# Grouped-query attention on one core: weighted sums redistributed between the score tiles, VectorE's correction steps moved behind the copy of the transposes, V loaded over four jobs

## The chip, the cores and the metric

The kernel runs on one core of a Trainium2 chip. The core's engines run side by side, each with its own queue of instructions, which it works through in order: PE (TensorE, matmuls), DVE (VectorE), ACT (ScalarE), POOL (GpSimd) and SP (SyncE, which issues DMAs here). Data lies in HBM, in SBUF (128 partitions) or in PSUM, to which PE writes. The metric is the device time of one execution in microseconds (us), lower is better. Before the change the median of three runs is 431.78 us (431.51 to 432.28).

## What is computed

Q has shape (8, 512, 32, 64): batch, sequence, heads, dimension. K and V have 8 heads, and four heads of Q share one head of K and V:

```python
K_expanded = np.repeat(K, heads_per_group, axis=2)
V_expanded = np.repeat(V, heads_per_group, axis=2)
...
scores = np.einsum('bhqd,bhkd->bhqk', Q, K_expanded) * scale
weights = np.exp(scores - np.max(scores, axis=-1, keepdims=True))
weights = weights / (np.sum(weights, axis=-1, keepdims=True) + 1e-10)
...
output = np.einsum('bhqk,bhkd->bhqd', weights, V_expanded)
```

There is no mask. scale is 1/8.

## The kernel before

**Jobs.** `fast_path` works through 64 jobs. A unit `u` is a batch `b` and a pair `gp` of K/V heads; job `j` is unit `j // 2` and one head `g = j % 2` of the pair, with its four heads of Q as two pairs `i`. One batch is eight jobs. The scores are made transposed (keys on the partitions), so that their exponentials can be the stationary operand of the matmul with V without another transpose. The maximum isn't subtracted; instead the row sums and V are checked to be in bounds, and a slow general path, not run here, follows if they aren't.

**Tiles of a job.** A job has 16 score pieces of 128 keys x 512 queries. ScalarE takes 14 of them, two at a time, as seven tiles: `act_tile(j, n)` issues two matmuls (L209) into `s_ps`, of which there are two buffers, and one exponential (L227) from there into `pt`. The other two pieces go to VectorE. From job 10 on every second job is *wide*: VectorE takes three pieces, and ScalarE's tile 4 has one piece only. The other jobs are called narrow. A wide job is followed by a narrow one.

**VectorE's exponentials.** `exp_d` issues the matmuls of these pieces into `d_ps` and turns them into 16-bit integers `u` (L238), whose bits read as an approximate exponential. `exp_d2` cuts out the mantissa, `f` (L259). GpSimd makes a correction from it, `g` (L251) and `w` (L255); in jobs 0 to 2 and 63 VectorE does this itself. `exp_d4` adds `u` and `w` into `pt` (L272); for job `j` this stands in job `j + 1`. The two steps `f` and `pt` read and write only SBUF.

**PSUM for it.** `d_ps` has one buffer of two banks. A job uses it twice: for the pieces of `exp_d`, then for the transposes of a later job's Q (`trans_q`, L164, copied to `qt` at L167), in the first batch also for K's (`first_k`), and, when `g` is 0, for a check of V (`check_v`, L177, reduced into `okv` at L184). The third piece of a wide job is put into its second bank in the job before.

**Weighted sums.** For job `j - 1`, called `last`, `pv(last, i, lo, hi)` issues matmuls `lo` to `hi` of 32 for head pair `i` (L303), each with a block of `pt` as the stationary operand and 65 columns of V, the last of which is ones and gives the row sum. `pv` has one buffer of two banks. The matmuls of pair 1 take the keys in the order 2, 3, 1, 0; a wide job's blocks from the 16th on, and a narrow job's from the 24th on, need `exp_d4`. `norm(last, i)` follows on VectorE: reciprocal `inv` (L336), product `o_sb` (L340), and after every second job the store by SP. After every eighth job (after pair 1 of jobs 7, 15, 23 ..., so at the end of jobs 8, 16, 24 ...) two small VectorE steps (L314) check 128 columns of `inv` against bounds; they read and write SBUF.

**Order.** The order is written out by hand, and each engine keeps it. In a job of the steady state PE's queue is, with n for `act_tile(j, n)`: 0, pieces of `exp_d`, 1, 11 weighted sums of pair 0, 2, 11 more, 3, 10 more, 4, transposes (and check, and the third piece of the next job), 5, 16 of pair 1, 6, 16 more. VectorE's queue is: `u`, `pt` of the last job, `f`, `norm` of pair 0, copy of the transposes, `okv`, the next job's third `u`, `norm` of pair 1. GpSimd issues the loads of Q, K and V as DMAs, from its own queue and ahead of the job's `g` and `w`: one load of Q per unit, in the third job of a batch the next batch's K, in the fourth its V as four loads of 128 KB. SP transposes the next batch's K by DMA in the fifth job (`dma_k`).

Of the kernel before, what the change touches and what calls it, by code (L numbers as in the profile page):

```python
# [11 lines left out]
FP32 = mybir.dt.float32  # L12
BF16 = mybir.dt.bfloat16
FP16 = mybir.dt.float16
I16 = mybir.dt.int16
U16 = mybir.dt.uint16
I32 = mybir.dt.int32
ALU = mybir.AluOpType
# [15 lines left out]
VV_HI = 1.0e30  # L34
# [24 lines left out]
def fast_path(ctx, tc, Q, K, V, out, flag):  # L59
    nc = tc.nc  # L60
    B, S, H, D = Q.shape
    KV = K.shape[2]
    HPG = H // KV
    SC = S // 128
    GP = KV // 2
    NU = B * GP
# [6 lines left out]
    const_pool = ctx.enter_context(tc.tile_pool(name="const", bufs=1))  # L73
# [13 lines left out]

    ident = const_pool.tile([128, 128], BF16, name="ident")
    ok = const_pool.tile([128, SPB * 2 * SC], FP32, name="ok")
    okv = const_pool.tile([128, NU + 1], FP32, name="okv")  # L90
    okall = const_pool.tile([128, 1], FP32, name="okall")
    gate = const_pool.tile([1, 1], FP16, name="gate")
    warm = const_pool.tile([128, S], BF16, name="warm")
# [6 lines left out]
    def load_k(b, lo=0, hi=KV):  # L100
        if b not in kn:
            kn[b] = knat_pool.tile([128, SC, KV, D], BF16, name="k_nat")
        nc.gpsimd.dma_start(
            out=kn[b][:, :, lo:hi, :],
            in_=K[b, :, lo:hi, :].rearrange("(sc p) g d -> p sc g d", p=128),
        )


    def load_v(b, lo=0, hi=KV):
        for sc in range(SC):  # L110
            nc.gpsimd.dma_start(  # L111
                out=vt[b % 2][:, sc, lo:hi, 0:D],
                in_=V[b, sc * 128:(sc + 1) * 128, lo:hi, :],
            )
# [16 lines left out]
    def d_tile():  # L131
        return d_pool.tile([128, 2, S], FP32, name="d_ps")
# [60 lines left out]
    def taken(j):  # L193
        return 3 if WIDE(j) else 2
# [22 lines left out]
    def open_job(j):  # L217
        pt = pt_pool.tile([128, NPAIR, SC, 2, S], FP16, name="pt")
        jobs.setdefault(j, {}).update(pt=pt, pv={})

    def act_tile(j, n):
        group = act_tiles(j)[n]
        i, kc, lo = group[0]
        ps = s_pool.tile([128, 2, S], FP32, name="s_ps")
        for _, _, m in group:
            scores(j, ps[:, m, :], i, kc, m)
        nc.scalar.activation(  # L227
            out=jobs[j]["pt"][:, i, kc, lo:, :], in_=ps[:, lo:, :], func=EXP, scale=scale
        )

    def exp_d(j, lo, hi, ps):
        st = jobs.setdefault(j, {})
        if "u" not in st:
            for name, dtype in (("u", I16), ("f", I16), ("g", BF16), ("w", BF16)):
                st[name] = dve_pool.tile([128, 3, S], dtype, name=name + "16")[:, 0:taken(j), :]
        for n in range(lo, hi):
            scores(j, ps[:, n - lo, :], DPAIR, n // 2, n % 2)
        return lambda: nc.vector.tensor_scalar(  # L238
            out=st["u"][:, lo:hi, :], in0=ps[:, 0:hi - lo, :], scalar1=A_U, scalar2=B_U,
            op0=ALU.mult, op1=ALU.add,  # L240
        )


    def by_pool(j):
        return 3 <= j < NJOB - 1
# [3 lines left out]
    def correction(engine, f, g, w):  # L249
        as_bits = engine is nc.gpsimd  # L250
        engine.tensor_scalar(  # L251
            out=g, in0=f, scalar1=-EXP_F1, scalar2=EXP_K * 2.0 ** (24 * as_bits),
            op0=ALU.add, op1=ALU.mult,
        )
        engine.tensor_tensor(out=w, in0=g, in1=f.bitcast(FP16) if as_bits else f, op=ALU.mult)  # L255

    def exp_d2(j):
        st = jobs[j]
        nc.vector.tensor_single_scalar(  # L259
            out=st["f"], in_=st["u"], scalar=1023, op=ALU.bitwise_and  # L260
        )
        if by_pool(j):
            exp_d3(j, nc.gpsimd)

    def exp_d3(j, engine):
        st = jobs[j]
        correction(engine, st["f"], st["g"], st["w"])

    def exp_d4(j):
        st = jobs[j]  # L270
        n = taken(j)
        nc.vector.tensor_tensor(  # L272
            out=st["pt"][:, DPAIR, :, :, :].rearrange("p kc m q -> p (kc m) q")[:, 0:n, :].bitcast(
                U16
            ),
            in0=st["u"],
            in1=st["w"],
            op=ALU.add,
        )
# [8 lines left out]
    def pv(j, i, lo, hi):  # L288
        st = jobs[j]
        u, g = divmod(j, 2)  # L290
        b, gp = divmod(u, GP)
        if lo == 0:

            if j < NJOB - 1:
                t = pv_pool.tile([128, 2, S], FP32, name="pv")
            else:
                t = d_tile() if i == 0 else s_pool.tile([128, 2, S], FP32, name="s_ps")
            t = t.rearrange("p m (qc c) -> p m qc c", qc=SC)
            st["pv"][i] = t[:, :, :, 0:D + 1]
        order = blocks(j, i)  # L300
        for n in range(lo, hi):
            kc, m, qc = order[n]
            nc.tensor.matmul(  # L303
                st["pv"][i][:, m, qc, :],
                st["pt"][:, i, kc, m, qc * 128:(qc + 1) * 128],
                vt[b % 2][:, kc, 2 * gp + g, :],
                start=(n < 2 * SC and qc == 0),
                stop=(n >= len(order) - 2 * SC and qc == SC - 1),
            )
# [73 lines left out]
        )  # L383


    def probe():
        f = const_pool.tile([128, 2], I16, name="probe_f")
        g = const_pool.tile([128, 2], BF16, name="probe_g")
        w = const_pool.tile([128, 2], BF16, name="probe_w")
        nc.gpsimd.memset(f, 512)  # L390
        correction(nc.gpsimd, f, g, w)
        nc.vector.tensor_scalar(
            out=okv[:, NU:NU + 1], in0=w[:, 0:1], scalar1=-80.0, scalar2=2.0 * VV_HI,
            op0=ALU.is_gt, op1=ALU.mult,
        )


    load_k(0, 0, 2)
    load_q(0, (0, 2, 4, 8))
    make_identity(nc, ident)  # L400
# [13 lines left out]
    bank = d_tile()  # L414
# [4 lines left out]
    bank = d_tile()  # L419
# [3 lines left out]
    for j in range(NJOB):  # L423
        end = j == NJOB - 1
        last = j - 1
        late = last >= 0
        u, g = divmod(j, 2)
        b, gp = divmod(u, GP)
        open_job(j)
        if j == 1:  # L430

            nc.gpsimd.tensor_copy(out=gate, in_=jobs[0]["pt"][0:1, 0, SC - 1, 0, 0:1])
            load_q(2)
            load_q(3)
            probe()
        if g == 0 and u >= 1 and u + 3 < NU:
            load_q(u + 3)
        if gp == 1 and b + 1 < B:
            if g == 0:
                load_k(b + 1)  # L440
            else:
                load_v(b + 1)
        if gp == 2 and g == 0 and b + 1 < B:
            dma_k(b + 1)
        act_tile(j, 0)
        if j == 0:
            trans_q(0, bank[:, 1, :], 1, NPAIR)()
            act_tile(j, 1)
            exp_d(j, 0, 2, d_tile())()
        else:  # L450
            exp_d(j, 0, 2, d_tile())()
            act_tile(j, 1)
        if late:
            pv(last, 0, 0, 11)
        act_tile(j, 2)
        if late and by_pool(last):
            exp_d4(last)
        exp_d2(j)
        if late:
            pv(last, 0, 11, 22)  # L460
        act_tile(j, 3)
        if late:
            pv(last, 0, 22, 32)
            norm(last, 0)
        act_tile(j, 4)

        reads = []
        if not end:
            bank = d_tile()

            ahead = (j + 1,) if j < 7 else (8, 9) if j == 7 else (j + 2,)
            for n, to in enumerate(ahead):
                if to < NJOB:
                    reads.append(trans_q(to, bank[:, n, :]))
            if j == 1:
                for swap in range(2):
                    reads.append(first_k(1, swap, bank[:, 1, swap * S // 2:]))
            elif j > 1 and b == 0 and gp + 1 < GP:
                reads.append(first_k(gp + 1, g, bank[:, 1, :]))
            if g == 0 and u > 0:  # L480
                reads.append(check_v(u - 1, bank[:, 1, S // 2:]))
            if j == NJOB - 2:
                reads.append(check_v(u, bank[:, 1, S // 2 + D:]))
            if taken(j + 1) > 2:
                reads.append(exp_d(j + 1, 2, taken(j + 1), bank[:, 1:2, :]))
        else:
            pv(j, 0, 0, 16)
        for read in reads:
            read()
        if not by_pool(j):  # L490
            exp_d3(j, nc.vector)
            exp_d4(j)
        act_tile(j, 5)
        if late:
            pv(last, 1, 0, 16)
        act_tile(j, 6)
        if late:
            pv(last, 1, 16, 32)
            norm(last, 1)
            del jobs[last]  # L500
        if end:
            pv(j, 0, 16, 32)
            norm(j, 0)
            pv(j, 1, 0, 32)
            norm(j, 1)
# [118 lines left out]
```

## Time and profile before

| What | Value |
|---|---|
| median of 3 runs | 431.78 us (431.51 to 432.28) |
| profiled execution | 433.24 us |
| its span, first to last instruction | 431.6 us |
| granted TensorE clock, mean | 0.995 |
| ACT busy | 407.5 us, 94% |
| PE busy | 395.4 us, 92% |
| DVE busy | 337.0 us, 78% |
| POOL busy | 292.7 us, 68% |
| exponentials L227 | 448, 406.2 us busy, 15.8 us idle before them |
| weighted sums L303 | 178.7 us busy |
| moved by DMA | 66.97 MB, mean 155 GB/s |

The span is what the profile's rows add up to; the profiled execution's time also has what lies around it, and the median is that of other executions. A row of the timeline has a start, a length, the engine, the line, the operation, what it writes and reads, how many instructions are merged into it, and in brackets the engine's idle time before it and what ended it. Rows of PE overlap, because matmuls are pipelined: the distance between two starts tells more than a length.

### The profile page before, as it was taken

To read this page: it belongs to the slowest core of one execution; us is meant where nothing else is said; L and a number is where in the kernel's file an instruction comes from. 1 tells how busy PE (TensorE), PEld (TensorE's weight loads), DVE (VectorE), ACT (ScalarE), POOL (GpSimd) and SP (SyncE) were. 2 spreads that over 40 slices of the span, in tenths; PEclk is the share of its full clock that TensorE was granted. 3 is DMA by queue.
4 is the path that set the end of the run, shared out by engine and by line. 5 is a ranking of instruction groups with operands and counts; after the bars stand their busy time and mean duration, and the time that the engine had idled before them with its cause. 6 is when DMAs were issued, how large, how long until landed. Compare 5 with 4: busy or idle time off the path is not lost.

```text
span 431.6 us, 13558 instructions
## 1 busy us (share of the span) xinstructions
PE 395.4 (92%) x5945; PEld 245.1 (57%) x5945; DVE 337.0 (78%) x612; ACT 407.5 (94%) x449; POOL 292.7 (68%) x212
## 2 busy tenths in 40 slices
PE   7888999999999999999999999999999999999994
PEld 2455565555556555556555556556555555655653
DVE  1687778878888878878878877887887887887875
ACT  2989999999999999999999999999999999999993
POOL 8805564896679776697676977599666987657650
PEclk9999999999999999999999999999999999999997
DMA  9998656799349966399846989569975998622214
GB/s 105 185 151 183 169 141 145 131 172 235 117 136 197 177 165 150 107 218 147 236 81 149 193 134 260 141 108 172 202 169 145 188 156 196 150 99 99 99 62 140
DMA packets 91439, 66.97 MB, mean 155 GB/s; under 512 B 52080, under 2 KB 74608, under 8 KB 91376
## 3 DMA queue, kind: packets, MB, share of 16 engines
q0 software_dynamic: 56544, 25.17, 50.4%
q1 hardware_dynamic: 34832, 40.90, 34.5%
q8 instruction: 47, 0.77, 0.8%
q14 instruction: 16, 0.13, 0.1%
HBM read 50.33 MB, written 33.55 MB: 194 GB/s over the span
## 4 chain that ended last, share of the span: by engine, by line
ACT 48%; PE 37%; DVE 10%; issue 3%; POOL 1%; ACTq 0%; DVEq 0%; POOLq 0%
ACT pt L227 48%; PE s_ps L209 15%; PE pv L303 11%; PE d_ps L164 8%; DVE o_sb L340 3%; DVE u L238 2%; PE d_ps L177 2%; PE d_ps L209 2%; DVE ok L314 1%; DVE pt L272 1%; DVE f L259 1%; DVE inv L336 1%; DVE w L255 0%; POOL q_nat L126 0%; DVE qt L167 0%
## 5 line engine op out<-in xcount | busy, mean ns | idle before, releaser
L227 ACT ACTIVATE pt<-s_ps 128x1024 f16<-128x1024 f32 (+1 forms) x448 | 406.2, 1032 | 15.8 <-PE s_ps L209 15.5
L303 PEld LDWEIGHTS <-pt 128*128 128x128 f16 x4096 | 142.7, 98 | 89.5 <-issue 57.1
L303 PE MATMUL pv<-v,pt 128*128 128x65 bf16 x4032 | 178.7, 195 | 9.0 <-DVE o_sb L340 4.6
L209 PE MATMUL s_ps<-qt,kt 64*128 64x512 bf16 x757 | 157.4, 382 | 15.6 <-ACT pt L227 1.8
L255 POOL TENSOR_TENSOR w<-g,f 128x1024 bf16<-128x1024 bf16 (+1 forms) x60 | 153.8, 2564 | 5.0
L251 POOL TENSOR_SCALAR g<-f 128x1024 bf16<-128x1024 int16 (+1 forms) x60 | 74.0, 1234 | 118.6 <-DVE f L259 118.2
L238 DVE TENSOR_SCALAR u<-d_ps 128x1024 int16<-128x1024 f32 (+1 forms) x91 | 96.0, 1055 | 0.7 <-PE d_ps L209 0.7
L340 DVE TENSOR_TENSOR o_sb<-pv,inv 128x512 f32<-128x512 f32 x125 | 86.4, 691 | 4.3
L209 PEld LDWEIGHTS <-kt 64*128 64x128 bf16 x896 | 55.1, 93 | 51.4 <-issue 18.5
L336 DVE RECIPROCAL inv<-pv 128x8 f32<-128x8 f32 x125 | 25.8, 206 | 52.7 <-PE pv L303 51.8
L167 DVE COPY qt<-d_ps 128x1024 bf16<-128x1024 bf16 (+1 forms) x65 | 44.2, 682 | 25.1 <-PE d_ps L177 11.6
L272 DVE TENSOR_TENSOR pt<-u,w 128x1536 uint16<-128x1536 int16 (+1 forms) x64 | 50.9, 795 | 0.3
L164 PE MATMUL d_ps<-ident,q_nat 128*128 128x128 bf16 x512 | 40.6, 224 | 0.9 <-DVE kt_first L146 0.9
L164 PEld LDWEIGHTS <-q_nat 128*128 128x128 bf16 x512 | 29.4, 99 | 20.3 <-issue 19.1
L259 DVE TENSOR_SCALAR f<-u 128x1536 int16<-128x1536 int16 (+1 forms) x64 | 32.1, 501 | 0.1
L209 PE MATMUL d_ps<-qt,kt 64*128 64x512 bf16 x139 | 31.7, 378 | 0.0
L111 POOL DMA_DIRECT2D v<-in_V_dram x32 | 28.2, 889 | 0.0
L126 POOL DMA_DIRECT2D q_nat<-in_Q_dram x34 | 27.3, 804 | 0.3 <-DMA q_nat<-in_Q_dram 0.3
L209 PE MATMUL s_ps<-qt,kt_first 64*128 64x512 bf16 x112 | 24.4, 431 | 2.6 <-ACT pt L227 1.1
L209 PEld LDWEIGHTS <-kt_first 64*128 64x128 bf16 x128 | 7.6, 96 | 10.9 <-issue 6.7
L177 PE MATMUL d_ps<-v 128*64 128x64 bf16 x256 | 10.4, 201 | 0.0
L177 PEld LDWEIGHTS <-v 128*64 128x64 bf16 x256 | 6.9, 110 | 3.5 <-issue 0.4
(46 smaller groups left out, 56.1 us busy)
## 6 DMA issues: line engine op xcount, KB each, us to landing
out_dram<-o_sb SPq DMA_DIRECT2D x31, 1024.0 KB, 5.3
q_nat<-in_Q_dram POOLq DMA_DIRECT2D x31, 512.0 KB, 7.0
k_nat<-in_K_dram POOLq DMA_DIRECT2D x7, 512.0 KB, 7.5
v<-in_V_dram POOLq DMA_DIRECT2D x28, 128.0 KB, 8.2
kt<-kt SPq DMA_DIRECT2D x14, 256.0 KB, 4.2
out_dram<-o_sb SPq DMA_DIRECT2D x4, 256.0 KB, 2.4
kt<-k_nat SPq DMA_TRANSPOSE x28, 7.6
v<-in_V_dram POOLq DMA_DIRECT2D x4, 96.0 KB, 7.7
```

Of the source, the lines that this page charges most:

```text
L164: nc.tensor.transpose(ps[:, i, sc, :], qn[u][:, sc, h:h + 2, :], ident)
L167: return lambda: nc.vector.tensor_copy(out=qt[u][:, g, lo:hi, :], in_=ps[:, lo:hi, :, :].rearrange("p i sc c -> p i (sc c)"))
L209: nc.tensor.matmul(ps, keys[64 * m:64 * m + 64, g ^ m, kc * 128:(kc + 1) * 128], qt[u][64 * m:64 * m + 64, g, i, :], start=True, stop=True,)
L227: nc.scalar.activation(out=jobs[j]["pt"][:, i, kc, lo:, :], in_=ps[:, lo:, :], func=EXP, scale=scale)
L238: return lambda: nc.vector.tensor_scalar(out=st["u"][:, lo:hi, :], in0=ps[:, 0:hi - lo, :], scalar1=A_U, scalar2=B_U, op0=ALU.mult, op1=AL ...
L251: engine.tensor_scalar(out=g, in0=f, scalar1=-EXP_F1, scalar2=EXP_K * 2.0 ** (24 * as_bits), op0=ALU.add, op1=ALU.mult,)
L255: engine.tensor_tensor(out=w, in0=g, in1=f.bitcast(FP16) if as_bits else f, op=ALU.mult)
L259: nc.vector.tensor_single_scalar(out=st["f"], in_=st["u"], scalar=1023, op=ALU.bitwise_and)
L272: nc.vector.tensor_tensor(out=st["pt"][:, DPAIR, :, :, :].rearrange("p kc m q -> p (kc m) q")[:, 0:n, :].bitcast(U16), in0=st["u"], in1=st ...
L303: nc.tensor.matmul(st["pv"][i][:, m, qc, :], st["pt"][:, i, kc, m, qc * 128:(qc + 1) * 128], vt[b % 2][:, kc, 2 * gp + g, :], start=(n < 2 ...
L336: nc.vector.reciprocal(out=inv, in_=sums[:, :, :, D:D + 1])
L340: nc.vector.tensor_tensor(out=osb[u][:, :, h:h + 2, :].rearrange("p qc m d -> p m qc d"), in0=sums[:, :, :, 0:D], in1=inv[:, :, :, None].t ...
```

## The change

The 64 matmuls of weighted sums per job stay, but are cut otherwise: pair 0 as 16 and 16 (after tiles 1 and 2), pair 1 as 11, 11 and 10 (after tiles 4, 5 and 6). The transposes with what belongs to them move from behind tile 4 to behind tile 3. VectorE's `pt` of the last job and `f` move behind the copy of the transposes and the `okv` step; so in GpSimd's queue `g` and `w` wait for a later `f`. The matmul of the next wide job's third piece, and its `u`, move from the transposes to behind tile 5. V's four loads are issued one per job in the fourth to the seventh job of a batch, instead of all in the fourth. A small probe of GpSimd's arithmetic in job 1 goes, with its column in `okv`.

```diff
-    okv = const_pool.tile([128, NU + 1], FP32, name="okv")
+    okv = const_pool.tile([128, NU], FP32, name="okv")
...
-    def load_v(b, lo=0, hi=KV):
-        for sc in range(SC):
+    def load_v(b, lo=0, hi=KV, chunks=range(SC)):
+        for sc in chunks:
...
-            probe()
         if g == 0 and u >= 1 and u + 3 < NU:
             load_q(u + 3)
-        if gp == 1 and b + 1 < B:
-            if g == 0:
-                load_k(b + 1)
-            else:
-                load_v(b + 1)
+        if (gp, g) == (1, 0) and b + 1 < B:
+            load_k(b + 1)
+        if 3 <= 2 * gp + g < 3 + SC and b + 1 < B:
+            load_v(b + 1, chunks=(2 * gp + g - 3,))
...
         if late:
-            pv(last, 0, 0, 11)
+            pv(last, 0, 0, 16)
         act_tile(j, 2)
-        if late and by_pool(last):
-            exp_d4(last)
-        exp_d2(j)
         if late:
-            pv(last, 0, 11, 22)
+            pv(last, 0, 16, 32)
+            norm(last, 0)
         act_tile(j, 3)
-        if late:
-            pv(last, 0, 22, 32)
-            norm(last, 0)
-        act_tile(j, 4)
...
-            if taken(j + 1) > 2:
-                reads.append(exp_d(j + 1, 2, taken(j + 1), bank[:, 1:2, :]))
         else:
             pv(j, 0, 0, 16)
         for read in reads:
             read()
+
+        if late and by_pool(last):
+            exp_d4(last)
+        exp_d2(j)
         if not by_pool(j):
             exp_d3(j, nc.vector)
             exp_d4(j)
+        act_tile(j, 4)
+        if late:
+            pv(last, 1, 0, 11)
         act_tile(j, 5)
+        if not end and taken(j + 1) > 2:
+            exp_d(j + 1, 2, taken(j + 1), bank[:, 1:2, :])()
         if late:
-            pv(last, 1, 0, 16)
+            pv(last, 1, 11, 22)
         act_tile(j, 6)
         if late:
-            pv(last, 1, 16, 32)
+            pv(last, 1, 22, 32)
             norm(last, 1)
```

More of the change, by code (lines that the diff above doesn't have):

```diff
@@ L383, in store @@
         )
[L386 to L395, printed above, removed]
     load_k(0, 0, 2)
```

## The prediction

> **What bounds the kernel now.** I read the page's busy shares first, then ScalarE's timeline, then PE's, VectorE's and GpSimd's for one pair of jobs, then the tile `ok`.
>
> ```profile
> PE 395.4 (92%) x5945; PEld 245.1 (57%) x5945; DVE 337.0 (78%) x612; ACT 407.5 (94%) x449; POOL 292.7 (68%) x212
> ACT 48%; PE 37%; DVE 10%; issue 3%; POOL 1%; ACTq 0%; DVEq 0%; POOLq 0%
> ```
>
> ScalarE (94%) and PE (92%) share the chain. ScalarE's timeline shows where it waits:
>
> ```profile
> 199.49 10.68 ACT L227 ACTIVATE pt<-s_ps 128x1024 f16<-128x1024 f32 x12
> 213.18 1.02 ACT L227 ACTIVATE pt<-s_ps 128x1024 f16<-128x1024 f32 x1
> 213.18 9.27 ACT L227 ACTIVATE pt<-s_ps 128x1024 f16<-128x1024 f32 x10
> 210.36 12.57 ACT L227 ACTIVATE pt<-s_ps 128x1024 f16<-128x1024 f32 x14 [0.19 <-PE s_ps L209]
> 223.13 7.50 ACT L227 ACTIVATE pt<-s_ps 128x1024 f16<-128x1024 f32 x8 [0.20 <-PE s_ps L209]
> 236.22 12.58 ACT L227 ACTIVATE pt<-s_ps 128x1024 f16<-128x1024 f32 x14 [0.19 <-PE s_ps L209]
> ```
>
> Rows two and three give the pitch of a full tile: (9.27 - 1.02) / 9 = 0.917. Row one is a first tile, ten more and the half tile of a wide job: 10.68 - 1.02 - 9.17 leaves 0.49 for that. A pair of jobs (narrow, wide) is 13 full tiles and one half: 12.41 on ScalarE alone. It takes 210.36 to 223.13 = 12.77. So 0.36 a pair is lost, 27 times, all of it after the half tile. The next pair, 223.13 to 236.22, takes 13.09: 0.32 more, six times in the run, at jobs 17, 25 ... 57.
>
> PE around the half tile (job 28, wide):
>
> ```profile
> 207.90 0.39 PE L209 MATMUL s_ps<-qt,kt 64*128 64x512 bf16 x2
> 208.22 0.48 PE L303 MATMUL pv<-v,pt 128*128 128x65 bf16 x10
> 208.82 0.37 PE L209 MATMUL s_ps<-qt,kt 64*128 64x512 bf16 x1
> 209.12 0.62 PE L164 MATMUL d_ps<-ident,q_nat 128*128 128x128 bf16 x8
> 209.67 0.33 PE L177 MATMUL d_ps<-v 128*64 128x64 bf16 x8
> 209.93 0.39 PE L209 MATMUL s_ps<-qt,kt 64*128 64x512 bf16 x2
> 210.25 0.67 PE L303 MATMUL pv<-v,pt 128*128 128x65 bf16 x16
> 210.85 0.39 PE L209 MATMUL s_ps<-qt,kt 64*128 64x512 bf16 x2
> ```
>
> From start to start: a score pair 0.32, a half pair 0.30, 8 transposes 0.55, 8 check matmuls 0.26, 16 weighted sums 0.60. One more or less is 0.032 ((0.67 - 0.51) / 5, against the rows of 11), so 11 take 0.44 and 10 take 0.41. A tile's exponential ends 1.455 after its scores start (0.43 to its start, 1.02 long); scores wait for the end of the tile two before, plus 0.05. In steady state PE can therefore be 2 x 0.917 - 1.505 = 0.33 late before ScalarE feels it.
>
> Call E3 = 0 the end of tile 3 in a wide job. Today S4 = -0.87 (buffer), S5 = -0.87 + 0.30 + 0.55 + 0.26 = 0.24, so tile 5 ends at 1.70 where ScalarE could have had 1.41; two stretches of 16 (0.92 each) add the rest of the 0.36. The rule reproduces the pair to 0.01.
>
> **The change, part by part.** *PE.* In the new order S1 = -3.62 (buffer), S2 and S3 each 0.92 later, S4 = -1.77 + 0.32 + 0.55 + 0.26 = -0.64, S5 = -0.64 + 0.30 + 0.44 = 0.10. Tile 5 ends at 1.56: 0.16 lost instead of 0.36. After it stand 11 and 10 matmuls, so PE has caught up by the next job. Gain: 0.20 a pair.
>
> *VectorE and GpSimd.* `pt` (L272) and `f` (L259) move behind the copy, so `f`, and GpSimd's `g` and `w` after it, come later within the job. With job start S0 = 0, in a wide job: S3 = 2.76, check matmuls at 3.63, copy 0.38 later at 4.02, `okv` 4.63, `pt` 4.76, `f` 5.36 to 5.91, `g` 6.01 to 7.48, `w` 7.56 to 10.66 (spacings of the rows at 207.39 to 210.66). The next job begins at 6.14, so in its frame `w` ends at 4.52, its `pt` (0.95) at 5.50, and the weighted sums from block 16 may go at 5.56. PE reaches block 16 at 5.28. The 0.28 it waits puts S6 0.34 late, beside 0.33 of slack: 0.01 a pair. That leaves 0.19 x 27 = **-5.1 us**, with a sharp edge: each further 0.1 in this chain costs 2.7 us. From `w` to `pt` I took 0.03 (`probe_w` ends 16.39, its reader starts at 16.42).
>
> *The bounds check.* Eight times a second small step of VectorE, L314 twice, follows the second `norm` of a job. This is what decides my number:
>
> ```profile
> 221.41 1.46 POOL L251 TENSOR_SCALAR g<-f 128x1536 bf16<-128x1536 int16 x1 [2.17 <-DVE f L259]
> 222.96 3.10 POOL L255 TENSOR_TENSOR w<-g,f 128x1536 bf16<-128x1536 bf16 x1
> 225.50 1.03 DVE L314 SCALAR_TENSOR_TENSOR ok<-inv,ok 128x128 f32<-128x128 f32 x2
> 226.45 1.22 DVE L238 TENSOR_SCALAR u<-d_ps 128x1024 int16<-128x1024 f32 x1
> ...
> 15.64 0.69 DVE L272 TENSOR_TENSOR pt<-u,w 128x1024 uint16<-128x1024 int16 x1
> ...
> 15.74 0.65 POOL L255 TENSOR_TENSOR probe_w<-probe_g,probe_f 128x2 bf16<-128x2 bf16 x1
> ```
>
> The two L314 are alike, yet the median is 0.29 and the longest 0.71. The long one starts at 225.50 inside `w` and ends 0.15 after `w` does (226.06); so in all six wide cases, and at job 9, with GpSimd idle, both take 0.29. The other way round, two elements of `probe_w` took 0.65 because VectorE's `pt` ran until 16.33. So a VectorE step with two SBUF operands and a GpSimd step that reads SBUF exclude each other, each for the whole of the other. Today only the last 0.56 of `w` is left to wait for.
>
> [...]
>
> After the change, at the end of such a wide job: next S0 6.14, `inv` 6.25, `o_sb` 6.49, first L314 at 7.10. `g` runs 6.01 to 7.48, so it waits and ends at 7.63. `w` stands ready at 7.56, starts at 7.63, and the second L314, which comes 0.03 after the first, waits for all of `w`: until 10.87. Then `u` ends at 12.01, which is 5.87 in the new job. `d_ps` has one buffer, so the transposes, now at 3.08, wait until 5.93: 2.85 late, S4 2.8 late, ScalarE 2.48. Behind it `norm`, the copy and `pt` follow on VectorE until 8.20, block 16 waits another 0.3, S6 is 3.04 late: ScalarE loses 2.7 instead of 0.32. Six times: **+14.3**. At jobs 8 and 9 (both narrow) L314 at 7.37 falls into `w` (7.01 to 9.14): the transposes 1.3 late, 1.3 - 0.33 = **+1.0**.
>
> *V.* One load occupies GpSimd for 0.88. Behind a wide `w` (ends 4.52) it is done at 5.40, before `f` at 5.84; in the other two jobs, behind `w` (2.8) and a Q load (0.81), by 4.5, before 5.91. Hidden. Four at once would have reached 8.0. The last piece leaves in job 6, lands 8.2 later in job 7, and is first read in job 9; SP's queue is not touched. If that cover went, GpSimd's chain would pay as above.
>
> *Start and end.* In the first batch K's transposes stand with Q's: S1 to S4 becomes 0.92 + 0.92 + 1.46, 0.22 lost at job 4 against 0.17 now; in job 3, where VectorE has until then done the whole correction itself, tile 4 comes 0.24 later, and jobs 1 and 2 give about as much as job 0 takes. Between -0.5 and +0.7; I take **+0.3**, the sum of the worked jobs. The removed probe (0.15 on VectorE, 1.0 on GpSimd) is waited for by nobody. In job 63 the last L314 at 3.7 meets `w` (until 4.58), and `pt` of jobs 62 and 63 now follow it: the last `pt` ends 8.65 after S0 where it ended 7.10: **+1.5** (0.7 without the meeting).
>
> Sum: -5.1 + 14.3 + 1.0 + 0.3 + 1.5 = **+12.0**. The profiled execution took 433.24 (span 431.6), so it would take 445.2; the median of the runs, 431.78, becomes **443.8**.
>
> **Rivals.** (1) *The second L314 reaches the port ahead of `w`.* GpSimd's start at 0.08 after `g` may hide a late first read. Then `w` begins about 0.4 late, an event costs 0.39, and the sum is -5.1 + 0.4 + 1.0 + 0.3 + 1.5 = -1.9: **429.9**, faster. It decides in a gap of 0.15: `w` ready at 0.08 after `g`, the second step at 0.18 and, by the 0.15 a freed step needs of its 0.29, at the port 0.14 later. That is why I put it behind. (2) *No meeting*: `g` does not hold L314 off, or only operands as large as `w`'s do. Against it: `probe_g`, the same operation, also ended only 0.05 after a VectorE step. Sum -5.1 - 1.9 + 0.3 + 0.7 = -6.0: **425.8**. (3) *Worse*: the chain from `f` to `pt` is 0.1 to 0.2 longer than I think, in 27 pairs: **446.5 to 449.2**. (4) *The pieces cancel*: half the events take rival 1's way and the chain gains nothing: near 432 to 438.
>
> **Chances.** Forecast (440 to 446) 0.64, rival 1 0.16, rival 2 0.06, rival 3 0.10, rival 4 0.04. The range must reach rival 1 to leave out no more than 0.2: 428.5 to 447.5; the likeliest case alone is 440 to 446. About 0.2% is what a measurement tells from no change: faster 0.22, within 0.02, slower 0.76.
>
> **What will show it.** Right: a second L314 of about 3.2 us at jobs 17, 25 ... 57, ending 0.15 after `w`; ScalarE idle some 2.7 there; other pairs at 12.58, tile 5 of wide jobs 0.16 late. Rival 1: both L314 under 0.6 and `w` starting 0.4 after `g`. Rival 3: pairs over 12.65 with PE waiting for `pt` in every narrow job. Wrong altogether: `f` not near 5.4 after S0, since every later time hangs on it.

## The result and the profile after

The kernel after the change takes 448.39 us (median of 4 runs, 447.62 to 450.54), beside 431.82 (431.51 to 432.28) for the kernel before on the same chip: 1.0391 times as long, 95% interval 1.0354 to 1.0428. It is slower, as forecast, and 0.9 us beyond the upper end of the range. The profiled execution took 448.15, its span 446.5, 14.9 more than the 431.6 of before.

The page of the kernel after: busy shares, the clock in 40 slices, and the chain by engine.

```profile
PE 396.1 (89%) x5945; PEld 241.6 (54%) x5945; DVE 355.4 (80%) x611; ACT 407.0 (91%) x449; POOL 292.3 (65%) x209
...
PEclk8699999999989999699999999999998999989998
...
PE 46%; ACT 36%; DVE 12%; issue 3%; POOL 2%; ACTq 0%; DVEq 0%; POOLq 0%
```

PE and ScalarE did the same work in a longer span. VectorE is the one whose busy time rose, by 18.4 us (337.0 before), although it lost a step: a step that waits for GpSimd counts as busy (the second check below is 3.145 long; in run 1, where GpSimd is idle beside them, no check takes more than 0.293). What the prediction and the expectations call the port is a name for this: steps of VectorE and GpSimd that hold each other up, read from the lengths of their rows. What the two engines share there no run shows. The clock row has dips in mid-run; the mean granted clock is 0.961. The kernel before has none there (mean 0.995):

```profile
PEclk9999999999999999999999999999999999999997
```

ScalarE's timeline of the kernel after, jobs 25 to 41 (start, length, instructions merged, idle time before):

```profile
181.87 1.02 ACT L227 ACTIVATE pt<-s_ps 128x1024 f16<-128x1024 f32 x1 [2.87 <-PE s_ps L209]
183.13 1.02 ACT L227 ACTIVATE pt<-s_ps 128x1024 f16<-128x1024 f32 x1 [0.23 <-PE s_ps L209]
184.81 1.02 ACT L227 ACTIVATE pt<-s_ps 128x1024 f16<-128x1024 f32 x1 [0.66 <-PE s_ps L209]
186.07 47.72 ACT L227 ACTIVATE pt<-s_ps 128x1024 f16<-128x1024 f32 x53 [0.23 <-PE s_ps L209]
236.03 50.70 ACT L227 ACTIVATE pt<-s_ps 128x1024 f16<-128x1024 f32 x56 [2.24 <-PE s_ps L209]
```

Where the kernel before stopped after every half tile, 53 and 56 exponentials now run without a gap over 0.15 (the view merges rows with smaller ones): the recut does what it was costed at (a pair takes 12.59, was 12.77). Between these stretches stand single holes, 2.24 to 2.87 and what follows them. They lie in jobs 17, 25, 33, 41, 49 and 57, which take 9.79, 10.85, 9.01, 10.07, 9.92 and 9.71 instead of 6.42.

One of them, at the turn from job 32 to job 33, in VectorE's timeline:

```profile
228.44 0.56 DVE L259 TENSOR_SCALAR f<-u 128x1536 int16<-128x1536 int16 x1
...
229.60 0.69 DVE L340 TENSOR_TENSOR o_sb<-pv,inv 128x512 f32<-128x512 f32 x1
230.21 3.67 DVE L314 SCALAR_TENSOR_TENSOR ok<-inv,ok 128x128 f32<-128x128 f32 x2
233.80 1.21 DVE L238 TENSOR_SCALAR u<-d_ps 128x1024 int16<-128x1024 f32 x1
```

and in GpSimd's, at the same time:

```profile
229.09 1.46 POOL L251 TENSOR_SCALAR g<-f 128x1536 bf16<-128x1536 int16 x1 [2.50 <-DVE f L259]
230.64 3.09 POOL L255 TENSOR_TENSOR w<-g,f 128x1536 bf16<-128x1536 bf16 x1
```

The pair of checks takes 3.67 us; by the tile's rows the first is 0.489 long, the second 3.145. The first outlasts `g` (ends 230.55) by 0.14, the second outlasts `w` (ends 233.73) by 0.15. Job 33 begins with its scores at 229.25 and job 32 6.17 earlier, at 223.08, so `f` stands at 5.36, `g` at 6.01, `w` at 7.56 and the checks at 7.13 after the start of job 32, where the prediction had 5.36, 6.01, 7.63 and 7.10. It was the first forecast way, not rival 1, in six cases of six (second checks of 3.142 to 3.145):

```profile
L314 DVE SCALAR_TENSOR_TENSOR ok<-inv,ok x16: 258/490/3145, 70.2 to 435.3; 128x128 f32<-128x128 f32 x14, 128x104 f32<-128x104 f32 x2
```

(16 instructions, then the shortest, median and longest in ns.) What the prediction had no term for is seen in PE's timeline, here in job 25 and at the same place in job 33:

```profile
177.22 0.39 PE L209 MATMUL s_ps<-qt,kt 64*128 64x512 bf16 x2
180.28 1.01 PE L164 MATMUL d_ps<-ident,q_nat 128*128 128x128 bf16 x8 [2.67 <-DVE u L238]
181.22 0.61 PE L209 MATMUL s_ps<-qt,kt 64*128 64x512 bf16 x2
...
232.00 0.39 PE L209 MATMUL s_ps<-qt,kt 64*128 64x512 bf16 x2
235.06 0.61 PE L164 MATMUL d_ps<-ident,q_nat 128*128 128x128 bf16 x8 [2.67 <-DVE u L238]
235.60 0.39 PE L209 MATMUL s_ps<-qt,kt 64*128 64x512 bf16 x2
```

PE is idle for 2.67 us in both, waiting for `u`. In job 25 the transposes then take 1.01 instead of 0.61 and a score pair 0.61 instead of 0.39. The windows of the kernel after (each 3.40 us: busy time and instructions of PE, PEld, DVE, ACT, POOL, then granted clock, DMA share, GB/s) tell why:

```profile
179.20:182.60 3.40, 2.32 (x23) 1.60 (x23) 3.10 (x5) 0.73 (x1) 0.00 (x0) 0.51 0.01 2
182.60:186.00 3.40, 3.40 (x30) 1.67 (x30) 1.81 (x5) 2.35 (x3) 2.61 (x2) 0.50 0.02 5
235.00:238.40 3.40, 3.20 (x49) 1.94 (x49) 3.21 (x7) 2.25 (x3) 0.67 (x1) 1.00 0.00 1
```

After the hole in job 25 the granted clock is half (0.51, 0.50) and PE, though busy throughout, issues 30 matmuls where after the hole in job 33 it issues 49 in the same time. Job 33 is the only one of the six with no half clock, and the shortest.

### The profile page after: what moved, and what is told of

The parts are those of the page before. It is cut to its first block, busy times and chain, and to the rows that moved or that the text cites. A ratio compares the mean times of both kernels' runs of the same rounds, so it can differ in the third digit from the quotient of the medians.

```text
span 446.5 us, 13581 instructions
## 1 busy us (share of the span) xinstructions
PE 396.1 (89%) x5945; PEld 241.6 (54%) x5945; DVE 355.4 (80%) x611; ACT 407.0 (91%) x449; POOL 292.3 (65%) x209
## 4 chain that ended last, share of the span: by engine, by line
PE 46%; ACT 36%; DVE 12%; issue 3%; POOL 2%; ACTq 0%; DVEq 0%; POOLq 0%
ACT pt L227 36%; PE pv L303 20%; PE s_ps L209 18%; PE d_ps L164 5%; DVE ok L314 3%; DVE o_sb L340 2%; DVE u L238 2%; PE d_ps L177 2%; DVE pt L272 1%; PE d_ps L209 1%; POOL w L255 1%; DVE qt L167 1%; DVE inv L336 1%; DVE w L255 0%; POOL q_nat L126 0%
## 5 line engine op out<-in xcount | busy, mean ns | idle before, releaser
L303 PEld LDWEIGHTS <-pt 128*128 128x128 f16 x4096 | 146.7, 99 | 89.5 <-issue 60.7
L303 PE MATMUL pv<-v,pt 128*128 128x65 bf16 x4032 | 186.0, 197 | 4.5 <-DVE o_sb L340 1.8
L209 PEld LDWEIGHTS <-kt 64*128 64x128 bf16 x896 | 47.5, 94 | 56.2 <-issue 29.2
L209 PE MATMUL d_ps<-qt,kt 64*128 64x512 bf16 x139 | 33.1, 392 | 0.0
L259 DVE TENSOR_SCALAR f<-u 128x1536 int16<-128x1536 int16 (+1 forms) x64 | 30.5, 477 | 0.0
L314 DVE SCALAR_TENSOR_TENSOR ok<-inv,ok 128x128 f32<-128x128 f32 (+1 forms) x16 | 24.7, 1543 | 0.3
## 6 DMA issues: line engine op xcount, KB each, us to landing
v<-in_V_dram POOLq DMA_DIRECT2D x28, 128.0 KB, 7.2
```

The source lines that it names most:

```text
L209: nc.tensor.matmul(ps, keys[64 * m:64 * m + 64, g ^ m, kc * 128:(kc + 1) * 128], qt[u][64 * m:64 * m + 64, g, i, :], start=True, stop=True,)
L259: nc.vector.tensor_single_scalar(out=st["f"], in_=st["u"], scalar=1023, op=ALU.bitwise_and)
L303: nc.tensor.matmul(st["pv"][i][:, m, qc, :], st["pt"][:, i, kc, m, qc * 128:(qc + 1) * 128], vt[b % 2][:, kc, 2 * gp + g, :], start=(n < 2 ...
L314: nc.vector.scalar_tensor_tensor(out=out_, in0=inv, scalar=bound, in1=in1, op0=op, op1=ALU.mult)
```

## The experiments

**Theory.** The whole loss is the meeting of L314 with `g` and `w`, in two parts: VectorE's checks wait for GpSimd (3.67 the pair) and hold back PE's transposes (2.6 a time), and PE's idleness then costs it the clock (0.50 to 0.51 after the hole in job 25). **Rivals**: (a) the recut or the later `pt` and `f` cost time of themselves, by the chain from `f` to `pt`; (b) the clock drops for another reason, or costs nothing beside the wait; (c) V's spread loads are what matters. In every ratio below the kernel before ran on the same chip.

**1. The checks moved.** The change stays; the two checks of a batch go behind the next job's copy and `pt`, when GpSimd is idle.

```diff
-            in_bounds((ok[:, 0:cols], ok[:, 0:cols]), flat, ok[:, 0:cols])
+            if n == SPB - 1:
+                checks.append(lambda: in_bounds((ok[:, 0:cols], ok[:, 0:cols]), flat, ok[:, 0:cols]))
+            else:
+                in_bounds((ok[:, 0:cols], ok[:, 0:cols]), flat, ok[:, 0:cols])
...
             exp_d4(last)
+        while checks:
+            checks.pop()()
         exp_d2(j)
```

> The changed kernel, with only the bounds check (L314 twice, after every eighth job) put between pt and f of the following job, where w of the last job has ended and g of this one has not begun. Theory (the shared SBUF port makes the second L314 wait for all of w, PE stands still behind it and its clock halves): both L314 under 0.6 us, no stall at jobs 17, 25 ... 57, granted clock above 0.99, pairs of jobs still 12.59: 431.8 - 5.0 - 1.9 + 0.3 + 0.7 = about 426. Rival (the clock drops come from the new rhythm of PE, not from the stalls): the clock stays near 0.96 and the time near 431. Rival (the loss sits in the recut weighted sums): above 440.

Measured: 427.76 (427.07 to 428.44), ratio 0.9902 (0.9885 to 0.9919). The tile's row:

```profile
L314 DVE SCALAR_TENSOR_TENSOR ok<-inv,ok x16: 256/285/293, 74.2 to 414.1; 128x128 f32<-128x128 f32 x14, 128x104 f32<-128x104 f32 x2
```

No check is longer than 0.293, the six jobs take 6.42, and from 20 us after the start to the last 5 us no stretch has half the clock. (The stretches outside keep the mean granted clock at 0.982 here and at 0.986 to 0.989 in runs 2 to 4, below the 0.99 that I expected.) Moving two instructions of 0.29 took 20.6 us off. The 1.7 above the expectation is partly seen: the wide job after each event takes 6.35 instead of 6.16. The checks now stand ahead of `f`, the next job's third `u` and the second `norm` on VectorE; that `norm` begins 0.2 later (6.11 after the start of job 17 on ScalarE, 5.91 in run 4), and the wide job's first weighted sums wait for its `o_sb`: 6 x 0.19 = 1.1.

**2. Filling PE's idle time.** The change stays and L314 meets `w` as before, but PE gets 55 matmuls of constant data, whose results nothing reads, ahead of the transposes of the six jobs.

```diff
+        fill = None
+        if j > 16 and j % 8 == 1:
+            fill = s_pool.tile([128, 2, S], FP32, name="s_ps")
+            for _ in range(55):
+                nc.tensor.matmul(fill[:, 0, 0:D + 1], warm[:, 0:128], warm[:, 0:D + 1], start=True, stop=True)
...
-        act_tile(j, 4)
+        act_tile(j, 4, fill)
```

> The changed kernel, with 55 matmuls of 65 columns whose result nobody reads, put ahead of the transposes in jobs 17, 25 ... 57 (into the score buffer of tile 4, before its scores): PE has work in most of the 2.7 us in which it stood still. The collision stays: the second L314 still 3.14 us. Theory (part of the loss is PE's clock, halved after the idle stretch): granted clock back above 0.99, each of the six jobs 9.0 us as job 33 has it, not 9.7 to 10.8: about 443, 5 below the changed kernel. Rival (the clock halves for another reason, or costs nothing): clock about 0.96 and 448 or a little more.

Measured: 442.67 (442.39 to 442.87), ratio 1.0245 (1.0225 to 1.0265). PE in job 25, and the tile's row:

```profile
177.21 1.83 PE L452 MATMUL s_ps<-warm 128*128 128x65 bf16 x55 [0.52 <-ACT pt L228]
179.36 0.61 PE L164 MATMUL d_ps<-ident,q_nat 128*128 128x128 bf16 x8 [0.32 <-DVE u L239]
...
L315 DVE SCALAR_TENSOR_TENSOR ok<-inv,ok x16: 254/487/3153, 70.1 to 429.5; 128x128 f32<-128x128 f32 x14, 128x104 f32<-128x104 f32 x2
```

The wait for `u` is still there and the second check still takes 3.15, but PE sits idle for 0.52 ahead of the filling and 0.32 behind it instead of 2.67, the clock stays full in all six jobs (in job 25 the 8 transposes take 0.61, not 1.01; the mean granted clock is 0.986, not 0.961), and each of the six jobs takes 9.00 or 9.01, what job 33 took. Useless work made the kernel 448.39 - 442.67 = 5.7 us faster: that is the clock's part, and rival (b) is out.

**3. `pt` and `f` put back.** The change otherwise stays: `exp_d4(last)` and `exp_d2(j)` return to behind tile 2, ahead of `norm` of pair 0, so that GpSimd runs earlier.

```diff
         act_tile(j, 2)
+        if late and by_pool(last):
+            exp_d4(last)
+        exp_d2(j)
...
-        if late and by_pool(last):
-            exp_d4(last)
-        exp_d2(j)
```

> The changed kernel, with VectorE's pt and f put back ahead of the norm of pair 0 (after tile 2), all else as changed: the weighted sums as 16, 16, 11, 11, 10, the transposes behind tile 3, V over four jobs. Theory (only the later f, which moves w under the check, costs): the long L314 back to 0.71, no stall, clock above 0.99, pairs 12.57 since pt is early again: 431.8 - 5.4 + 0.3 + 0.3 = about 427. Rival (the recut or V's loads cost): 435 or more.

Measured: 431.62 (431.07 to 433.83), ratio 0.9995 (0.9979 to 1.001): 4.6 above what I expected. VectorE's timeline at job 17:

```profile
119.55 0.69 DVE L340 TENSOR_TENSOR o_sb<-pv,inv 128x512 f32<-128x512 f32 x1
120.16 1.32 DVE L314 SCALAR_TENSOR_TENSOR ok<-inv,ok 128x128 f32<-128x128 f32 x2
121.40 1.22 DVE L238 TENSOR_SCALAR u<-d_ps 128x1024 int16<-128x1024 f32 x1
```

and GpSimd's:

```profile
117.91 3.10 POOL L255 TENSOR_TENSOR w<-g,f 128x1536 bf16<-128x1536 bf16 x1
```

I had taken over the 0.71 of the kernel before, but the job around it is shorter now: when the check arrives, `w` (until 121.01) has 0.85 to go, not 0.56, and the check is 0.99 long. That costs not 0.32 but 1.2, in six jobs of 7.53 (7.2 us in all). The recut has the transposes a tile earlier, so that less of VectorE's delay is hidden; run 5 below parts the 1.2. The pairs without an event take 12.585, as after the change: the late `pt` and `f` are neither needed for that gain nor a loss in it. Rival (a) falls for these jobs.

**4. Checks with one SBUF operand.** The change stays; the two checks stand where they stood, as a minimum and a maximum of `inv` into two small tiles, which are compared with the bounds once at the end. A `tensor_reduce` reads one operand, where L314 reads two.

```diff
-            in_bounds((ok[:, 0:cols], ok[:, 0:cols]), flat, ok[:, 0:cols])
+            nc.vector.tensor_reduce(out=low[:, k:k + 1], in_=flat, op=ALU.min, axis=AX.X)
+            nc.vector.tensor_reduce(out=high[:, k:k + 1], in_=flat, op=ALU.max, axis=AX.X)
...
```

> The changed kernel, with the two L314 of a check replaced at the same place by two reductions of the same 128 columns (minimum and maximum, each with one SBUF operand), compared with the bounds once at the end; three small steps more in job 63. [...] Rival (any VectorE step on SBUF waits for GpSimd): the second reduction 3.1 us and 443 to 449.

Measured: 426.56 (426.44 to 426.65), ratio 0.987 (0.9851 to 0.989). I had expected about 426.5, with no stall and both reductions at 0.3. VectorE's timeline at job 17:

```profile
121.08 0.27 DVE L355 TENSOR_REDUCE low<-inv 128x1 f32<-128x128 f32 x1
121.27 0.28 DVE L356 TENSOR_REDUCE high<-inv 128x1 f32<-128x128 f32 x1
```

and GpSimd's:

```profile
119.96 1.46 POOL L253 TENSOR_SCALAR g<-f 128x1536 bf16<-128x1536 int16 x1 [2.50 <-DVE f L261]
121.51 3.10 POOL L257 TENSOR_TENSOR w<-g,f 128x1536 bf16<-128x1536 bf16 x1
```

The first runs wholly inside `g`, the second starts inside it and ends after `w` has begun, and neither is held: 0.27 and 0.28. The six jobs take 6.42 to 6.43, and the clock has no dip in mid-run (mean 0.989). Same place, same queue, same input: what is gone is the second operand and, as a reduction writes one column, the result of 128 columns, and with them 448.39 - 426.56 = 21.8 us. This is the clearest of the runs, though it doesn't part the two.

**5 and 6. The same checks in the two other orders.** Run 5 is run 3 with the reductions of run 4 instead of L314; run 6 is the kernel before with them. Run 5 has the diffs of runs 3 and 4, run 6 that of run 4.

> Both at once: pt and f early as in e3, and the check as two reductions as in e4. In e3 the six jobs 17, 25 ... 57 took 7.53 us and not 6.32, because the long L314 had grown from 0.71 to 0.99 there. Theory (that 1.2 is the wait for w at the port, and nothing else): each falls back to 6.32, 7 us below e3: 424.5. Rival (the 1.2 comes from VectorE's longer queue between u and norm): above 429.

> The kernel before the change, with only the check as two reductions at its old place. Theory: the 0.32 a time that jobs 17, 25 ... 57 lose goes, and nothing else: 431.8 - 1.9 + 0.4 for the steps added in job 63 = 430.2. Rival (the check's place matters little before the change, other waits end last there): 431.8 or more. Beside e4 it gives what the recut is worth without any collision: theory 3.5 to 4.

Measured: run 5 426.18 (425.78 to 427.37), ratio 0.9859 (0.9836 to 0.9881), 1.7 above what I expected; run 6 430.59 (429.85 to 431.22), ratio 0.9951 (0.9931 to 0.997). ScalarE in run 6:

```profile
209.45 12.57 ACT L229 ACTIVATE pt<-s_ps 128x1024 f16<-128x1024 f32 x14 [0.20 <-PE s_ps L211]
222.22 12.57 ACT L229 ACTIVATE pt<-s_ps 128x1024 f16<-128x1024 f32 x14 [0.20 <-PE s_ps L211]
```

These are the pairs that the prediction showed at 12.77 and 13.09: both are 12.77 now, so the 0.32 at every eighth job was this wait too. Run 5's six jobs take 6.67, not 6.32: with no step waiting for `w`, two reductions and `u` in one queue still hold the transposes back by 0.35, so that of run 3's 1.2 some 0.86 was the wait for `w`. The three orders, with the checks as they were and as reductions:

| order | L314 | reductions |
|---|---|---|
| before | 431.8 | 430.6 |
| after, with `pt` and `f` put back (runs 3 and 5) | 431.6 | 426.2 |
| after | 448.4 | 426.6 |

Runs 5 and 6 ran on a chip on which the kernel before took 432.4, so the ratios are the better measure. In the right column, where no check waits for GpSimd, the rest of the change is worth 3.5 to 4 us (ratios of 0.987 and 0.9859 against 0.9951). In the left one it is worth nothing or costs 16.6. The order of `pt` and `f` decides mainly what the checks meet; besides, the early order saves 0.9 us in jobs 2 and 3 (13.72 in run 5, 14.64 in run 4) and 0.9 from job 63 on (13.67 and 14.58).

**7. V's loads at once.** Run 4, with V's four loads in one job again.

```diff
-        if 3 <= 2 * gp + g < 3 + SC and b + 1 < B:
-            load_v(b + 1, chunks=(2 * gp + g - 3,))
+        if (gp, g) == (1, 1) and b + 1 < B:
+            load_v(b + 1)
```

> e4 with V's four loads in one job again, as before the change. Theory (GpSimd is then late for the f of that job by 2.2 us, w of the next job by some 0.2, and pt has no slack): about 0.25 in each of seven batches, 428. Rival (hidden by slack): 426.6 as e4.

Measured: 428.73 (427.62 to 429.05), ratio 0.9908 (0.9888 to 0.9927), 2.2 above run 4, which ran on another chip (1.6 by the ratios). The intervals touch (run 4 up to 0.989, run 7 from 0.9888), so the size is taken from the trace: jobs 13, 21 ... 53 take 6.63 to 6.66 instead of 6.42, some 0.23 six times or 1.4 us. GpSimd at job 19:

```profile
137.37 3.60 POOL L113 DMA_DIRECT2D v<-in_V_dram  x4
141.04 1.04 POOL L253 TENSOR_SCALAR g<-f 128x1024 bf16<-128x1024 int16 x1
```

The four issues fill GpSimd's queue for 3.60 and `g` starts straight behind them, without a wait for `f`. Spread, they are hidden, as the prediction had it, and rival (c) is out as a cause of the loss: spreading them gains.

**8. Only `pt` and `f` late, in the order of before.** From the other side: the kernel before, with these two steps alone behind the copy, and the third piece of the next job after them.

```diff
         act_tile(j, 2)
-        if late and by_pool(last):
-            exp_d4(last)
-        exp_d2(j)
...
-            if taken(j + 1) > 2:
-                reads.append(exp_d(j + 1, 2, taken(j + 1), bank[:, 1:2, :]))
...
             read()
+        if late and by_pool(last):
+            exp_d4(last)
+        exp_d2(j)
+        if not end and taken(j + 1) > 2:
+            exp_d(j + 1, 2, taken(j + 1), bank[:, 1:2, :])()
```

> The kernel before the change, with only VectorE's pt and f moved behind the copy of the transposes, at the old cut of the weighted sums (the third piece of a wide job follows them; its buffers demand it). Theory (the later f alone makes the collision, and the late pt costs where the recut does not make room): the second L314 3.1 us again, 3 to 4 us lost in each of six jobs as in the changed kernel (and the clock under 0.97), PE waiting for pt of wide jobs some 0.5 to 0.7: 450 to 460. Rival (the recut is needed for the collision): near 432.

Measured: 483.66 (483.18 to 484.75), ratio 1.1177 (1.115 to 1.1204), far above what I expected. The events are as in the kernel after; VectorE's timeline in one of them:

```profile
189.40 3.98 DVE L314 SCALAR_TENSOR_TENSOR ok<-inv,ok 128x128 f32<-128x128 f32 x2
```

Two rows of the waits, with their sum, number and the longest:

```profile
ACT pt L227 <- PE s_ps L209: 57.6, 75, 6.9
...
PE d_ps L209 <- DVE qt L167: 21.3, 27, 0.8
```

The miss is elsewhere: a pair without an event takes 13.59, not 12.77, 27 times 0.82 or 22 us. The third piece's matmuls wait for the copy (the second row: 27 times), and every narrow job takes 7.13 instead of 6.35. The wait for `pt` that I had priced at 0.5 to 0.7 a pair came only 5 times, 3.1 us in all. So moved in this way alone the two steps cost more than the change; that the later place of the third piece and the earlier one of the transposes make room for them in the change is likely, but no run takes these away one by one.

**9. A version from this.** Run 5, with the reductions behind the copy of the next job, where the 0.35 goes as well.

```diff
+            def check():
+                nc.vector.tensor_reduce(out=low[:, k:k + 1], in_=flat, op=ALU.min, axis=AX.X)
+                nc.vector.tensor_reduce(out=high[:, k:k + 1], in_=flat, op=ALU.max, axis=AX.X)
...
         for read in reads:
             read()
+        while checks:
+            checks.pop()()
```

> e5 with the two reductions put behind the copy of the transposes of the following job. In e5 jobs 17, 25 ... 57 still took 6.67 and not 6.32, with no step waiting at the port: there the two reductions (0.47) stand ahead of u, pt, f and the norm that frees the weighted sums' buffer. Theory (a queue on VectorE, not the port): all jobs 6.32, about 2 us below e5: 424. Rival (the 0.35 has another cause): 426 as e5.

Measured: 424.41 (424.18 to 425.53), ratio 0.9816 (0.9789 to 0.9843), the fastest of all. ScalarE:

```profile
94.42 206.10 ACT L229 ACTIVATE pt<-s_ps 128x1024 f16<-128x1024 f32 x229
```

229 exponentials in 206 us without one gap that the view would show (over 0.15), across all events between: no job has a stall of its own, and they alternate between 6.33 and 6.26. That is 12.59 a pair, what run 4 has too (346.2 from job 8 to job 63 in both): the 2 us below run 4 are not in the steady state but in jobs 2 and 3, at the end, and in the first microseconds.

**10. `f` early in wide jobs only.** Run 4, with `f` of the wide jobs ahead of `norm` of pair 0, so that the longer correction is ready sooner.

```diff
         act_tile(j, 2)
+        if WIDE(j):
+            exp_d2(j)
...
-        exp_d2(j)
+        if not WIDE(j):
+            exp_d2(j)
```

> e4 with f of wide jobs alone put ahead of the norm of pair 0, as in e5; pt, and f of narrow jobs, stay behind the copy. w of a wide job then ends 2.5 us earlier, so pt of the wide job no longer waits for it, and PE no longer for pt. Theory (the 0.10 that narrow jobs lose in e4, 6.42 beside 6.32, is PE's wait for pt at block 16): narrow jobs 6.32, wide jobs between 6.16 and 6.26, pairs 12.48 to 12.58: 423.5 to 426.5. Rival (the 0.10 is PE's own work in the recut): pairs 12.59 and 426.6 as e4.

Measured: 434.42 (433.57 to 435.33), ratio 1.0045 (1.0027 to 1.0063): a miss, by some 8 us. VectorE's timeline around a wide job:

```profile
205.88 0.82 DVE L261 TENSOR_SCALAR f<-u 128x1536 int16<-128x1536 int16 x1
...
208.37 1.65 DVE L274 TENSOR_TENSOR pt<-u,w 128x1024 uint16<-128x1024 int16 x1
```

and GpSimd's:

```profile
204.16 2.13 POOL L257 TENSOR_TENSOR w<-g,f 128x1024 bf16<-128x1024 bf16 x1
...
208.01 1.47 POOL L253 TENSOR_SCALAR g<-f 128x1536 bf16<-128x1536 int16 x1
209.56 3.41 POOL L257 TENSOR_TENSOR w<-g,f 128x1536 bf16<-128x1536 bf16 x1
```

The narrow jobs fell to 6.32 to 6.35 as meant. But `f` meets the last job's `w` (0.82 long, elsewhere 0.55), `pt` meets `g` (1.65, elsewhere 0.68) and `w` meets `pt` (3.41, elsewhere 3.09): such meetings are now in nearly every pair, and 12 of the 27 wide jobs take 6.5 to 6.6 instead of 6.16, 12 more 6.2 to 6.4. In job 58 `pt` comes when `w` has just begun and waits for all of it (3.47), PE stands still for 2.3 and loses the clock for 6.8 (its mean over the run is 0.977): jobs 58 and 59 take 8.89 and 8.09, 4.5 us together, half of the miss in this trace.

## Why the prediction came out as it did

The direction, the mechanism, its place and its times were right; one large term of the sum was mis-sized, and the range had too little room for it. Against the span, which grew by 14.9:

| term | predicted | in the trace | from |
|---|---|---|---|
| pairs, 27 | -5.1 | -4.8 | 12.59 instead of 12.77 |
| meeting at jobs 17 to 57 | +14.3 | +19.1 | 21.05 lost with the job that follows, less 1.9 before |
| jobs 8 and 9 | +1.0 | +1.0 | 13.74 instead of 12.72 |
| start | +0.3 | -1.0 | to the start of job 8 |
| end | +1.5 | +0.5 | from the start of job 63, 14.48 instead of 13.99 |
| sum | +12.0 | +14.8 | |

**What bounds the kernel, and the pairs.** Right: 12.59 against 12.58. The chain from `f` to `pt` was costed well enough that rival 3 did not come: PE's wait for `pt` before a weighted sum (its number, and the longest) is there, 0.26 a time, as large as the 0.28 worked out.

```profile
PE d_ps L164 <- DVE u L238: 17.2, 7, 2.7
...
PEld L303 <- DVE pt L272: 6.0, 23, 0.6
```

**The bounds check, "ScalarE loses 2.7 instead of 0.32. Six times: +14.3".** This is the step that failed. That a check waits for the whole of `w` was my estimate, from a row of 0.71 that met only the last 0.56 of it; it held in every row (a second L314 of 3.14, 0.15 past the end of `w`; transposes 2.74 late, 235.06 less 232.32, where 2.85 was said), and its price holds where the clock does: job 33 lost 2.59, and in run 2 all six did. But the working assumed that PE takes up its work at the speed at which it left it. In five of six events it came back at half the clock (granted 0.50 to 0.51) for 3.4 or 6.8 us, and lost 3.37, 4.43, 3.65, 3.57 and 3.45. Together 21.05, 3.5 on the mean. Run 2 gives the clock's part on its own as 5.7; in the trace it is 21.05 - 6 x 2.59 = 5.5. The sign of this was on the page: the granted clock was 0.995 before, and the change was to put PE to rest for 2.7 us at a time, which the kernel before never did (PE's longest rests there are 1.33, in the first 25 us and at the end). It belonged in the range as a cost with two bounds: nothing, or slow matmuls after each hole, for which the kernel before has rows at its start, where PE comes from rest (4 transposes in 0.59, later 8 in 0.62).

**Jobs 8 and 9** were right: the first L314 there took 2.07, until 0.15 after `w`. (The rows of PE that the prediction calls job 28 are of job 30; nothing hangs on it.) **V** was right in that it is hidden; "four at once would have reached 8.0" is 2.2 us on GpSimd and, by run 7, only some 0.23 on ScalarE. **The start** differs by 0.8 in the first exponential alone (8.24 instead of 9.07). It goes with the speed of PE's matmuls: the first transposes of Q take 0.38 there and took 0.59 before. The kernels made from the changed one have this start at 8.24 to 8.66, runs 6 and 8 at 9.07 as before; whether the change has a hand in that, or chance, isn't shown. Chance is likelier. The traces of before and run 6, with the start at 9.07, have mean clocks of 0.995 and 0.996. Of the 17 executions of the kernel before that stand beside runs 1 to 4, four have 0.994 or 0.995 and spans of 431.3 to 431.5, ten have 0.986 to 0.990 and spans of 429.7 to 430.2; and run 1, made from the changed kernel, has an execution at 0.996, the longest of its six. Their starts were not traced, though. **The end** came out at a third, because the last check just missed: it started at 434.975, `w` ended at 435.054, and it took 0.258.

**From the span to the median.** The prediction carried the difference of two profiled executions over to the medians. The one of before was 1.4 above its median, the one of after 0.2 below: of the 16.6 between the medians, 1.7 comes from there and not from any term. If the start is a matter of chance, its -1.0 and these 1.7 are in the main one thing: the profiled execution of before was one with the late start. Without the 1.7 the terms would have put the median at 431.8 + 14.8 = 446.6, inside the range, but by luck: the 4.8 that the meeting cost beyond its price was partly made up by the start (1.3) and the end (1.0).

**The rivals.** Rival 1 (second check ahead of `w`), rival 2 (no meeting) and rival 4 are refuted by the six rows of 3.14, rival 3 by the 12.59. What the prediction never asked is whether the change had to pay at all: with the checks out of the way (runs 4 and 9) the same recut is faster than the kernel before.

What stays open: why PE's first matmuls are faster in some runs, and where exactly PE's idleness becomes enough for the clock to fall. No run varied that by itself, and behind stretches of 3.413 us that PE covered 0.63 (run 8) and 0.57 (run 10) the clock fell, while behind two that were covered as much in job 33 it did not.

## What to carry to other kernels

Before a step is moved, lay its new times beside everything on an engine whose steps the rows show to hold it up, here GpSimd for VectorE (0.71 instead of 0.29 before the change), down to the smallest rare step: two instructions of 0.29 us, eight times a run, turned a gain of some 4 us into a loss of 17. In a profile such a wait is not idle time, it is a step whose longest row is far above its median (before the change 0.708 and 0.294); the cure here was another operation (a reduction of one operand to one column) or another place, not less work. And a stall on PE is priced with the clock that comes after it, not by its length alone: holes of 2.67 us cost 2.59 with the clock kept and 3.37 to 4.43 with it halved.

## What the runs showed of the hardware

**The clock fell after 2.67 us of idleness.** Between its start and its end the kernel after has five stretches at half clock (granted 0.50). They begin at 128.0, 179.2, 288.5, 343.1 and 397.7 and last 3.4 us, or 6.8 the second time; the later four start 15, 47, 63 and 79 times 3.413 us after the first. So here the clock changed on a grid of that pitch, and the same hole of 2.67 us counted by how it lay on it: in the 3.413 us just before each drop PE's matmuls covered 0.22 to 0.52 of the time, while in job 33 the hole was split between two such stretches covered 0.57 and 0.63, and the clock stayed at 1.00. The 2.67 us of rest sufficed in five cases of six.

**VectorE and GpSimd held each other up, also at a step with one operand.** Besides L314, VectorE's `pt` waited for `g` (1.65 instead of 0.68), GpSimd's `w` for `pt` (3.41 instead of 3.09), and `f`, which reads one 16-bit operand, was held beside `w` (0.82 instead of 0.55), all three in run 10, while an f32 reduction of one operand was not (0.274 to 0.278 in run 4, at all six jobs).
